# Attention weights and v in float32, and the product with v of a pair's two heads as float32 products in two column groups

## The chip, the cores and the metric

The kernel runs on one core of one Trainium2 chip. The metric is the device time of one execution in microseconds; three runs of the kernel before took 1297.36, 1299.44 and 1304.59 us, median 1299.44 us. A core has a matrix engine (PE, with its weight loads shown as PEld), a vector engine (DVE), an activation engine (ACT), a general engine (POOL) and a queue that issues DMAs (SP). Each engine runs its own instructions in order. Matrix products land in PSUM, eight banks of 128 partitions by 512 float32 values; all other tiles lie in SBUF.

## The reference, cut to what matters

Two layers, each attention and then a gated MLP, on 512 positions of width 1024; 16 heads of width 64. Layer 0 uses stick-breaking attention, layer 1 forgetting attention (a softmax with decay). In both, a causal matrix of weights `a` (or `p`) of each head multiplies that head's `v`:

```python
def stick_breaking_attention(q, k, v):
    ...
        z = jnp.einsum('bhqd,bhkd->bhqk', qb, kb).astype(jnp.float32) * scale
        ...
        a = jnp.where(strict, jnp.exp(log_beta + after), 0.0)
        outs.append(jnp.einsum('bhqk,bhkd->bhqd', a.astype(vb.dtype), vb))
...
def reference(x, c, w_mod, ...):
    for i in range(DEPTH):
        ...
        qkv = jnp.einsum('bsd,de->bse', h, w_qkv[i])
        q, k, v = (split_heads(t) for t in jnp.split(qkv, 3, axis=-1))
        ...
        o = jnp.einsum('bse,ed->bsd', merge_heads(o), w_o[i])
        x = x + gt_a[:, None, :] * rmsnorm(o, g_mix_post[i])
        ...
```

All is float32.

## The kernel before, in words

Almost every product is made of parts. A float32 tile is split (`split`, L190 to L193) into a high part of a reduced type (`fp32r`), written by ACT, and a low part, the difference, written by DVE or POOL. `mm3` (L264 to L268) then issues three products, high by high, low by high and high by low, into one bank.

Each layer's attention works through 16 heads in 8 pairs (`attention`, L529). In step h the scores of head h are made: four score products for query blocks of 128 rows, each in two parts (`scores`, L388), from which ACT, DVE and POOL make the weights (`stick` L391 to L401: two sigmoids on ACT, a scan on DVE at L399, a product on POOL or DVE at L400; `fox` L403 to L415 in layer 1). The head before, h-1, is turned meanwhile: `transposed` (L417) lets PE transpose its weights into four banks `pa` (L424) of 512, 384, 256 and 128 columns, one for each block kb of 128 key positions, and `split` makes high and low parts `ah` and `al` of them. Then `weighted` (L434) multiplies with v: the four v tiles hold for each head 64 high and 64 low columns, 128 in all, as the stationary operand; the moving operand is `ah` (L439) and then `al` (L440). So the bank `po` holds the product with v's high part in 64 partitions and with its low part in the other 64; ACT copies one half out (L444), DVE adds the other (L445) into `of`, and after a pair's second head `split` makes `oh` and `ol` of it, which `project` later multiplies with w_o.

PE's and SP's orders are those of the program text; the order of ACT, DVE and POOL is set by a scheduler when the program is built. Between these steps PE is given other work in small units by a `Filler` (L508): queries and keys of later pairs (`proj`, tile `pqk`), later v (`values`, tile `pv`), and the first products with w_o. The table `UNITS` says how many units stand in each step h, and the calls of `fill` in `attention` spread them in twelfths over the step. In layer 0 a second stream, `Background`, makes the next modulation columns on DVE from weights `wm` that DMAs bring (`acc`, L143); its DVE instructions stand between those of the attention. The v tiles come from `keep_values` (L464), for the first two groups of layer 0 at the end of `begin`, for the others in `values`. Most tiles of 128 by 512 (`slot`) share 44 rooms.

Of the kernel before, what the change touches and what calls it, by code (L numbers as in the profile page):

```python
# [8 lines left out]
F32 = mybir.dt.float32  # L9
# [3 lines left out]
ALU = mybir.AluOpType  # L13
AX = mybir.AxisListType

P = 128
D = 1024
S = 512
NT = S // P
ND = D // P  # L20
NH = 16
HD = 64
# [15 lines left out]
def trunk(ctx, tc, x, c, w_mod, b_mod, g_mix_pre, g_mix_post, w_qkv, w_o, w_fg, b_fg,  # L38
          g_ffn_pre, g_ffn_post, w_gate, w_up, w_conv, b_conv, w_down, out):
    nc = tc.nc  # L40
# [6 lines left out]
    def nm(s):  # L47
        serial[0] += 1
        return f"{s}_{serial[0]}"

    def bank(s="b"):
        return pp.tile([P, 512], F32, tag="bank", name=nm(s), bufs=8)

    def slot(s, dt=F32R):
        return sb.tile([P, 512], dt, tag="slot", name=nm(s), bufs=NS)
# [59 lines left out]
    def conv_columns():  # L115
        ps = bank("pcol")
        for l in range(DEPTH):
            nc.tensor.transpose(ps[:, P * l : P * l + 88], rowsB[:88, P * l : P * l + P], idn[:88, :88])
        for l in range(DEPTH):
            nc.vector.tensor_copy(colB[l], ps[:, P * l : P * l + 88])  # L120
        yield
# [69 lines left out]
    def split(hi, lo, src, engine=None):  # L191
        nc.scalar.copy(hi, src)  # L192
        (engine or nc.vector).tensor_tensor(lo, src, hi.bitcast(F32), op=ALU.subtract)  # L193
# [147 lines left out]
    def proj(l, p, j, ht, scale, res, parts=((0, S),)):  # L341
        wh, wl = ws.need((l, "qk", p, j))
        ps = bank("pqk")
        for c0, c1 in parts:
            for d in range(ND):
                ds_ = slice(d * P, (d + 1) * P)
                mm3(ps[:, c0:c1], (wh[:, ds_], wl[:, ds_]), block(ht, d, c0, c1), d == 0, d == ND - 1)
                if c1 - c0 == S or d % 2:
                    yield
        res[p, j] = queries(ps, scale) if j == 0 else keys(ps, kl[p % 2])  # L350

    A, B = slice(0, HD), slice(HD, P)
    kl = []

    def queries(ps, scale):

        res = slot("qa"), slot("qb")
        for x_, own in zip(res, (A, B)):
            nc.scalar.activation(x_[own], ps[own], AF.Copy, scale=scale)
        for x_, own, other in ((res[0], A, B), (res[1], B, A)):  # L360
            nc.vector.scalar_tensor_tensor(x_[other], ps[own], scale, x_[own].bitcast(F32), op0=ALU.mult, op1=ALU.subtract)
        return res
# [20 lines left out]
    def scores(l, hd, qb, q, k):  # L383
        n = (qb + 1) * P
        qs = slice(qb * P, n)
        ps = bank("ps")
        for i in range(2):
            nc.tensor.matmul(ps[:, :n], q[hd][:, qs], k[hd][i][:, :n], start=i == 0, stop=i == 1)  # L388
        return ps, n

    def stick(ps, n):  # L391


        bt = slot("bt", F32)
        om = slot("om", F32) if n > MULN else ps
        nc.gpsimd.memset(bt[:, n - 1 : n], 0.0)
        nc.scalar.activation(bt[:, : n - 1], ps[:, : n - 1], AF.Sigmoid)
        nc.scalar.activation(ps[:, :n], ps[:, :n], AF.Sigmoid, scale=-1.0)
        nc.vector.tensor_tensor_scan(om[:, :n][:, ::-1], ps[:, :n][:, ::-1], zid[:, S - n :][:, ::-1], 0.0, op0=ALU.mult, op1=ALU.add)  # L399
        (nc.gpsimd if n > MULN else nc.vector).tensor_tensor(bt[:, : n - 1], bt[:, : n - 1], om[:, 1:n], op=ALU.mult)  # L400
        return bt  # L401

    def fox(ps, qb, cum):  # L403

        n = (qb + 1) * P
        t = slot("fx", F32)[:, :n]
        e = t if n > MULN else ps[:, :n]
        m, s, r = tiny("mx"), tiny("sm"), tiny("rc")
        nc.vector.tensor_tensor_reduce(
            e.rearrange("p (b k) -> p b k", k=P), ps[:, :n].rearrange("p (b k) -> p b k", k=P), cum(qb),  # L410
            1.0, BIG, op0=ALU.add, op1=ALU.min, accum_out=m)
        nc.scalar.activation(e, e, AF.Exp, scale=-1.0, bias=m, accum_out=s)
        nc.vector.reciprocal(r, s)
        nc.vector.tensor_scalar(t, e, r, None, op0=ALU.mult)
        return t  # L415

    def transposed(probs):  # L417

        res = {}
        for kb in range(NT):  # L420
            n = (NT - kb) * P
            ps = bank("pa")
            for qb in range(NT - 1, kb - 1, -1):
                nc.tensor.transpose(ps[:, (qb - kb) * P : (qb - kb + 1) * P], probs[qb][:, kb * P : (kb + 1) * P], idn)  # L424
            if kb == 1:
                shared = slot("ah"), slot("al")
            hi, lo = (slot("ah"), slot("al")) if kb in (0, 2) else shared
            o = 384 if kb == 3 else 0
            hi, lo = hi[:, o : o + n], lo[:, o : o + n]
            split(hi, lo, ps[:, :n])  # L430
            res[kb] = (hi, lo)
            yield res

    def weighted(h, vt, at, o):  # L434

        po = bank("po")
        for kb in range(NT):
            lhs = by_head(vt[h // 4, kb])[:, h % 4, :]
            nc.tensor.matmul(po[:, kb * P :], lhs, at[kb][0], start=kb == 0, stop=False)  # L439
            nc.tensor.matmul(po[:, kb * P :], lhs, at[kb][1], start=False, stop=kb == NT - 1)  # L440
            yield
        hi, lo, f = o
        own, other = ((A, B), (B, A))[h % 2]
        nc.scalar.copy(f[own], po[other])  # L444
        nc.vector.tensor_tensor(f[own], po[own], f[own], op=ALU.add)  # L445
        if h % 2:
            split(hi, lo, f)

    def by_head(v):

        return v.rearrange("p (h e) -> p h e", h=4)

    def values(l, g, t, ht, vt):

# [7 lines left out]
        keep_values(ps[:, :256], g, t, vt)  # L462

    def keep_values(ps, g, t, vt):  # L464
        vt[g, t] = slot("v")
        dst = by_head(vt[g, t])
        split(dst[:, :, :HD], dst[:, :, HD:], ps.rearrange("p (h e) -> p h e", h=4))

    def forget(ht):

# [54 lines left out]
    def drain(g):  # L525
        for _ in g:
            pass

    def attention(l, qk, vt, ot, filler, units, bg):  # L529


        get = cums_of.get(l)
        late, cums = None, {}
        for h in range(NH + 1):
            p, hd = divmod(h, 2)
            done = [0, 0]

            def fill(n=1):
                done[0] += n
                u = (units[h] * min(done[0], 12) + 11) // 12 - done[1]  # L540
                done[1] += u
                filler.run(u)

            if h < NH and hd == 0:
                ot.append((slot("oh"), slot("ol"), slot("of", F32)))
            if get and h < NH:
                for i in range(h, min(h + 2, NH)):
                    if i not in cums:
                        cums[i] = get(i)
            probs, at = {}, None  # L550
            turned = transposed(late[0]) if late else None
            for qb in range(NT - 1, -1, -1):
                if h < NH:
                    ps, n = scores(l, hd, qb, qk[p, 0], qk[p, 1])
                    probs[qb] = stick(ps, n) if l % 2 == 0 else fox(ps, qb, cums[h])
                    fill()
                if turned:
                    at = next(turned)
                    fill()
            fill(2)  # L560
            if late:
                drain(turned)
                for i, _ in enumerate(weighted(late[1], vt, at, ot[late[1] // 2])):
                    if i % 2:
                        fill()
            fill(12)
            late = (probs, h)
            with tc.high_priority(offset=-100):
                bg.step(3 if h > 1 else 0)


    def begin(vt, qk):
# [41 lines left out]
        part, xt, acc, H = {}, {}, [], S // 2  # L614
# [92 lines left out]
        for t in range(NT):  # L707
            n = t + 1
# [29 lines left out]
        for j in range(ND):  # L738
            n = j + 1
# [17 lines left out]
        qk[0, 0] = queries(acc[4], 0.125)  # L757
        qk[0, 1] = keys(acc[6], kl[0])
        ws.upto(1)
        for g in range(2):  # L760
            for t in range(NT):
                keep_values(acc[t][:, 256 * g : 256 * g + 256], g, t, vt)
        qk[1, 0] = queries(acc[5], 0.125)
        return ht

# [1 line left out]
    for l in range(DEPTH):  # L767
# [35 lines left out]
        gens, ot = [], []  # L803
        for p in range(1, NPAIR):
            if (l, p) == (0, 3):
                gens.append(conv_columns())
            gens += [proj(l, p, j, ht, s, qk) for j, s in ((0, scale), (1, None)) if (p, j) not in qk]
            if p % 2 == 0 and (p // 2, 0) not in vt:
                gens += [values(l, p // 2, t, ht, vt) for t in range(NT)]
        gens += [project(t, ps_) for ps_ in (range(3), range(3, 5)) for t in range(2)] + [project(2, range(3))]  # L810
        filler = Filler(gens)
# [63 lines left out]
        for f in range(2, NF):  # L875
            g, u = bank("pgu"), bank("pgu")
# [67 lines left out]
```

## Time and profile before

| | us |
|---|---|
| median of three runs | 1299.44 |
| the profiled execution, its own time | 1295.07 |
| its span, first to last instruction | 1293.3 |
| PE busy | 1245.4 |
| DVE busy | 801.4 |
| ACT busy | 618.4 |
| POOL busy | 277.7 |

Layer 0's attention lies at about 85 to 275 us of the span, layer 1's at about 690 to 895 us, and the MLPs at 330 to 690 and from 930 us on. Busy times of PE count a product as longer than its place in the pipe: the ends of products are modelled, so the distance between two starts is the price of one product in a row. Idle time of an engine is given with what released it; where an engine runs in order, an instruction that waits holds up all that stand behind it.

### The profile page before, as it was taken

The page shows a single profiled execution, that of the slowest core. Times are in us where ns is not written, and L with a number is a line of the kernel's source. Part 1 is how long each engine was busy: PE and PEld are TensorE (multiplying, and loading weights), DVE is VectorE, ACT ScalarE, POOL GpSimd, SP SyncE. Part 2 cuts the span into 40 slices and gives each one's busy share as a digit, 9 for nine tenths or more (in the row PEclk, how much of TensorE's full clock was granted, in tenths as well). Part 3 has the DMA queues.
Part 4 walks back from the last instruction along what each step waited for, and adds up shares of the span by engine and source line. Part 5 has one row for each costly group of instructions (what it writes and reads, how often), then busy time and mean ns, then how long its engine had stood idle before and what let it go on. Part 6 is the DMA issues. An engine that isn't in the chain of part 4 may idle for free.

```text
span 1293.3 us, 17081 instructions
## 1 busy us (share of the span) xinstructions
PE 1245.4 (96%) x6244; PEld 1048.1 (81%) x6244; DVE 801.4 (62%) x1447; ACT 618.4 (48%) x1182; POOL 277.7 (21%) x302
## 2 busy tenths in 40 slices
PE   5899998999999999999999999999999999999997
PEld 3677878789888888888887889987888888888886
DVE  7878898856878887422363766776685444442233
ACT  5576666757333333311365665675743333332121
POOL 3665444620000000000113654452100000000000
PEclk9999999999999999999999999999999999999999
DMA  8662534231577776333403433332273333333231
GB/s 266 211 192 86 169 115 140 82 113 41 190 244 243 242 229 215 98 98 98 150 16 93 154 103 110 115 100 81 65 226 108 95 95 97 98 98 98 98 98 66
DMA packets 174857, 169.19 MB, mean 131 GB/s; under 512 B 6937, under 2 KB 151729, under 8 KB 174773
## 3 DMA queue, kind: packets, MB, share of 16 engines
q1 hardware_dynamic: 174596, 168.04, 41.3%
q8 instruction: 49, 0.80, 0.2%
q14 instruction: 36, 0.29, 0.1%
q10 hardware_dynamic: 176, 0.07, 0.0%
HBM read 165.92 MB, written 2.16 MB: 130 GB/s over the span
## 4 chain that ended last, share of the span: by engine, by line
PE 74%; DVE 12%; ACT 5%; DMA 4%; issue 3%; POOL 2%; SPq 0%; DVEq 0%; POOLq 0%; ACTq 0%
PE pgu L267 11%; PE pgu L266 11%; PE pgu L268 11%; PE pd L266 6%; PE pd L268 6%; PE pd L267 6%; PE pqk L266 3%; PE pqk L268 3%; PE pqk L267 3%; PE ps L388 2%; PE pa L424 2%; DMA wm<-in_w_mod_dram 2%; PE pv L267 2%; PE pv L266 2%; PE pv L268 2%
## 5 line engine op out<-in xcount | busy, mean ns | idle before, releaser
L192 ACT CAST wh<-wf 128x1024 fp32r<-128x1024 f32 (+2 forms) x178 | 185.3, 1041 | 313.8 <-PE pgu L267 140.6
L193 DVE TENSOR_TENSOR wl<-wf,wh 128x1024 fp32r<-128x1024 f32 x122 | 149.2, 1223 | 215.8 <-ACT wh L192 213.6
L267 PE MATMUL pgu<-htl,wh 128*128 128x512 f32 (+1 forms) x736 | 276.4, 376 | 0.4 <-DVE htl L328 0.3
L266 PE MATMUL pgu<-hth,wh 128*128 128x512 f32 (+1 forms) x736 | 276.3, 375 | 0.0
L268 PE MATMUL pgu<-hth,wl 128*128 128x512 f32 (+1 forms) x736 | 276.2, 375 | 0.0
L267 PEld LDWEIGHTS pgu<-htl,wh 128*128 128x128 f32 x736 | 138.5, 188 | 25.6 <-DVE htl L328 0.8
L193 POOL TENSOR_TENSOR wl<-wf,wh 128x1024 fp32r<-128x1024 f32 (+3 forms) x56 | 132.1, 2363 | 124.8 <-ACT wh L192 115.4
L266 PEld LDWEIGHTS pgu<-hth,wh 128*128 128x128 f32 x736 | 138.5, 188 | 25.1
L268 PEld LDWEIGHTS pgu<-hth,wl 128*128 128x128 f32 x736 | 138.5, 188 | 25.1
L279 POOL TENSOR_TENSOR r<-v,mhalf 128x1 f32<-128x1 f32 x32 | 17.9, 558 | 447.8 <-DVE v L275 447.8
L266 PE MATMUL pd<-wh,yh 128*128 128x512 f32 x288 | 112.0, 389 | 0.0
L267 PE MATMUL pd<-wl,yh 128*128 128x512 f32 x288 | 112.0, 389 | 0.0
L268 PE MATMUL pd<-wh,yl 128*128 128x512 f32 x288 | 112.0, 389 | 0.0
L143 DVE SCALAR_TENSOR_TENSOR acc<-wm,csil,acc 128x1024 f32<-128x1024 f32 x74 | 97.4, 1316 | 16.6 <-DMA wm<-in_w_mod_dram 16.0
L266 PE MATMUL pqk<-hth,wh 128*128 128x512 f32 (+1 forms) x240 | 100.6, 419 | 0.1
L268 PE MATMUL pqk<-hth,wl 128*128 128x512 f32 (+1 forms) x240 | 94.0, 392 | 0.4 <-POOL wl L193 0.4
L267 PE MATMUL pqk<-htl,wh 128*128 128x512 f32 (+1 forms) x240 | 93.6, 390 | 0.0
L856 ACT ACTIVATE cv<-cv 128x512 f32<-128x512 f32 x44 | 27.8, 632 | 102.7 <-DVE cv L855 98.2
L266 PE MATMUL pv<-wh,hth 128*128 128x256 f32 (+1 forms) x224 | 71.0, 317 | 0.8 <-ACT hth L663 0.4
L267 PE MATMUL pv<-wl,hth 128*128 128x256 f32 (+1 forms) x224 | 67.8, 303 | 0.9 <-POOL wl L193 0.9
L268 PE MATMUL pv<-wh,htl 128*128 128x256 f32 (+1 forms) x224 | 67.8, 303 | 0.0
L192 ACT CAST ah<-pa 128x128 fp32r<-128x128 f32 (+3 forms) x128 | 53.7, 427 | 21.0 <-PE pa L424 20.3
(199 smaller groups left out, 2442.8 us busy)
## 6 DMA issues: line engine op xcount, KB each, us to landing
wm<-in_w_mod_dram SPq DMA_DIRECT2D x80, 512.0 KB, 4.8
wf<-in_w_ffn_gate_dram SPq DMA_DIRECT2D x44, 512.0 KB, 4.1
wf<-in_w_ffn_up_dram SPq DMA_DIRECT2D x44, 512.0 KB, 3.7
wf<-in_w_ffn_down_dram SPq DMA_DIRECT2D x44, 512.0 KB, 3.5
wf<-in_w_qkv_dram SPq DMA_DIRECT2D x41, 512.0 KB, 3.8
wm<-in_w_mod_dram SPq DMA_DIRECT2D x32, 256.0 KB, 4.2
wf<-in_w_o_dram SPq DMA_DIRECT2D x16, 512.0 KB, 3.4
cum<-cumd SPq DMA_DIRECT2D x16, 512.0 KB, 4.3
```

The source lines that it names most:

```text
L143: nc.vector.scalar_tensor_tensor(acc, w, csil[:, d : d + 1], acc, op0=ALU.mult, op1=ALU.add)
L192: nc.scalar.copy(hi, src)
L193: (engine or nc.vector).tensor_tensor(lo, src, hi.bitcast(F32), op=ALU.subtract)
L266: nc.tensor.matmul(ps, ah, bh, start=first, stop=False)
L267: nc.tensor.matmul(ps, ah, bl, start=False, stop=False)
L268: nc.tensor.matmul(ps, al, bh, start=False, stop=last)
L279: nc.gpsimd.tensor_tensor(r, v, mhalf, op=ALU.pow)
L388: nc.tensor.matmul(ps[:, :n], q[hd][:, qs], k[hd][i][:, :n], start=i == 0, stop=i == 1)
L424: nc.tensor.transpose(ps[:, (qb - kb) * P : (qb - kb + 1) * P], probs[qb][:, kb * P : (kb + 1) * P], idn)
L856: nc.scalar.activation(a, a, AF.Silu)
```

## The change

The weights and v are no longer split. `transposed` copies each bank `pa` into a float32 tile `at` (ACT alone). `keep_values` copies v as float32, 512 columns, that is eight heads, to a tile. `weighted` now runs once for a pair, after its second head: for each key block it issues two float32 products, one for each head, with 64 columns of v as the stationary operand and `at` as the moving one; the first head's result goes to partitions 0 to 63 of the bank `po` and the second's to 64 to 127, with the tile position (0, 0) or (0, 64). `split` then makes `oh` and `ol` straight from the bank. The copy and the addition into `of` and the tile itself are gone, as are the two calls of `fill` between the products.

```diff
             if kb == 1:
-                shared = slot("ah"), slot("al")
-            hi, lo = (slot("ah"), slot("al")) if kb in (0, 2) else shared
+                shared = slot("at", F32)
+            t = shared if kb % 2 else slot("at", F32)
             o = 384 if kb == 3 else 0
-            hi, lo = hi[:, o : o + n], lo[:, o : o + n]
-            split(hi, lo, ps[:, :n])
-            res[kb] = (hi, lo)
+            res[kb] = t[:, o : o + n]
+            nc.scalar.copy(res[kb], ps[:, :n])
             yield res
 
-    def weighted(h, vt, at, o):
+    def weighted(p, vt, at, o):
 
         po = bank("po")
         for kb in range(NT):
-            lhs = by_head(vt[h // 4, kb])[:, h % 4, :]
-            nc.tensor.matmul(po[:, kb * P :], lhs, at[kb][0], start=kb == 0, stop=False)
-            nc.tensor.matmul(po[:, kb * P :], lhs, at[kb][1], start=False, stop=kb == NT - 1)
-            yield
-        hi, lo, f = o
-        own, other = ((A, B), (B, A))[h % 2]
-        nc.scalar.copy(f[own], po[other])
-        nc.vector.tensor_tensor(f[own], po[own], f[own], op=ALU.add)
-        if h % 2:
-            split(hi, lo, f)
...
+            for hd in range(2):
+                e = P * (p % 4) + HD * hd
+                nc.tensor.matmul(po[HD * hd : HD * hd + HD, kb * P :], vt[p // 4, kb][:, e : e + HD], at[hd][kb],
+                                 start=kb == 0, stop=kb == NT - 1, tile_position=(0, HD * hd))
+        split(*o, po)
...
     def keep_values(ps, g, t, vt):
-        vt[g, t] = slot("v")
-        dst = by_head(vt[g, t])
-        split(dst[:, :, :HD], dst[:, :, HD:], ps.rearrange("p (h e) -> p h e", h=4))
+        if (g // 2, t) not in vt:
+            vt[g // 2, t] = slot("v", F32)
+        o = 256 * (g % 2)
+        nc.scalar.copy(vt[g // 2, t][:, o : o + 256], ps)
...
             if late:
                 drain(turned)
-                for i, _ in enumerate(weighted(late[1], vt, at, ot[late[1] // 2])):
-                    if i % 2:
-                        fill()
+                if hd == 0:
+                    weighted(p - 1, vt, ats, ot[p - 1])
+                    ats = {}
             fill(12)
...
-        for g in range(2):
-            for t in range(NT):
-                keep_values(acc[t][:, 256 * g : 256 * g + 256], g, t, vt)
+        for t in range(NT):
+            vt[0, t] = slot("v", F32)
+            nc.scalar.copy(vt[0, t], acc[t])
```

The first place is PE in layer 0 at the products with v of the first pair. In the kernel before they stand once for each head; these are those of the pair's second head (`po` is the bank they add into, `ah` and `al` the parts of the turned weights, `v` the four v tiles, `pqk` a filler's bank):

```order
L439 MATMUL po_1135<-ah_1043,v_774 128x512
L440 MATMUL po_1135<-al_1044,v_774 128x512
L439 MATMUL po_1135<-ah_1067,v_777 128x384
L440 MATMUL po_1135<-al_1068,v_777 128x384
L266 MATMUL pqk_1118<-hth_107,wh_891 128x512
L267 MATMUL pqk_1118<-htl_108,wh_891 128x512
L268 MATMUL pqk_1118<-hth_107,wl_892 128x512
L439 MATMUL po_1135<-ah_1099,v_780 128x256
L440 MATMUL po_1135<-al_1100,v_780 128x256
L439 MATMUL po_1135<-ah_1067,v_783 128x128
L440 MATMUL po_1135<-al_1068,v_783 128x128
```

In the changed kernel PE has at this place the only run of the pair, with the two heads' tiles `at` in turn:

```order
L439 MATMUL po_1092<-at_903,v_774 64x512
L439 MATMUL po_1092<-at_1007,v_774 64x512
L439 MATMUL po_1092<-at_925,v_776 64x384
L439 MATMUL po_1092<-at_1029,v_776 64x384
L439 MATMUL po_1092<-at_945,v_778 64x256
L439 MATMUL po_1092<-at_1059,v_778 64x256
L439 MATMUL po_1092<-at_925,v_780 64x128
L439 MATMUL po_1092<-at_1029,v_780 64x128
L266 MATMUL pqk_1076<-hth_107,wh_874 128x512
```

Sixteen products for the pair, each into all 128 partitions, have become eight, each into 64; the first head's run has moved to the second's, and the filler's unit that stood inside the run stands behind it.

The second place is DVE in layer 0 while the first head is turned and the second head's weights are made (`om` and `ps` of L399 are the scans, `al` the low parts of the turned weights, `acc` the background sum, `bt` the weights). The kernel before has:

```order
L399 SCALAR_TENSOR_TENSOR om_906<-ps_902,zid 128x512
L193 TENSOR_TENSOR al_921<-pa_915,ah_920 128x512
L143 SCALAR_TENSOR_TENSOR acc_1151<-wm_1157,csil,acc_1151 128x1024
L399 SCALAR_TENSOR_TENSOR om_931<-ps_927,zid 128x384
L193 TENSOR_TENSOR al_945<-pa_940,ah_944 128x384
L143 SCALAR_TENSOR_TENSOR acc_1151<-wm_1160,csil,acc_1151 128x1024
L399 SCALAR_TENSOR_TENSOR ps_951<-ps_951,zid 128x256
L193 TENSOR_TENSOR al_967<-pa_963,ah_966 128x256
L400 TENSOR_TENSOR bt_954<-bt_954,ps_951 128x255
L399 SCALAR_TENSOR_TENSOR ps_970<-ps_970,zid 128x128
L193 TENSOR_TENSOR al_945<-pa_982,ah_944 128x128
L400 TENSOR_TENSOR bt_973<-bt_973,ps_970 128x127
```

The changed kernel has on DVE at this place:

```order
L399 SCALAR_TENSOR_TENSOR om_889<-ps_885,zid 128x512
L143 SCALAR_TENSOR_TENSOR acc_1106<-wm_1109,csil,acc_1106 128x1024
L399 SCALAR_TENSOR_TENSOR om_912<-ps_908,zid 128x384
L143 SCALAR_TENSOR_TENSOR acc_1106<-wm_1112,csil,acc_1106 128x1024
L399 SCALAR_TENSOR_TENSOR ps_930<-ps_930,zid 128x256
L143 SCALAR_TENSOR_TENSOR acc_1106<-wm_1115,csil,acc_1106 128x1024
L400 TENSOR_TENSOR bt_933<-bt_933,ps_930 128x255
L399 SCALAR_TENSOR_TENSOR ps_947<-ps_947,zid 128x128
L400 TENSOR_TENSOR bt_950<-bt_950,ps_947 128x127
```

The four subtractions are gone; the scans and background sums stay in turn.

More of the change, by code (lines that the diff above doesn't have):

```diff
@@ L425, in transposed @@
             if kb == 1:
-                shared = slot("ah"), slot("al")
-            hi, lo = (slot("ah"), slot("al")) if kb in (0, 2) else shared
+                shared = slot("at", F32)
+            t = shared if kb % 2 else slot("at", F32)
             o = 384 if kb == 3 else 0
-            hi, lo = hi[:, o : o + n], lo[:, o : o + n]
-            split(hi, lo, ps[:, :n])
-            res[kb] = (hi, lo)
+            res[kb] = t[:, o : o + n]
+            nc.scalar.copy(res[kb], ps[:, :n])
             yield res
-    def weighted(h, vt, at, o):
+    def weighted(p, vt, at, o):
         po = bank("po")
         for kb in range(NT):
-            lhs = by_head(vt[h // 4, kb])[:, h % 4, :]
-            nc.tensor.matmul(po[:, kb * P :], lhs, at[kb][0], start=kb == 0, stop=False)
-            nc.tensor.matmul(po[:, kb * P :], lhs, at[kb][1], start=False, stop=kb == NT - 1)
-            yield
-        hi, lo, f = o
-        own, other = ((A, B), (B, A))[h % 2]
-        nc.scalar.copy(f[own], po[other])
-        nc.vector.tensor_tensor(f[own], po[own], f[own], op=ALU.add)
-        if h % 2:
-            split(hi, lo, f)
-    def by_head(v):
-        return v.rearrange("p (h e) -> p h e", h=4)
+            for hd in range(2):
[3 more added lines that the diff above has]
+        split(*o, po)
     def values(l, g, t, ht, vt):
@@ L532, in attention @@
         get = cums_of.get(l)
-        late, cums = None, {}
+        late, ats, cums = None, {}, {}
         for h in range(NH + 1):
@@ L544, in attention @@
             if h < NH and hd == 0:
-                ot.append((slot("oh"), slot("ol"), slot("of", F32)))
+                ot.append((slot("oh"), slot("ol")))
             if get and h < NH:
@@ L549, in attention @@
                         cums[i] = get(i)
-            probs, at = {}, None
+            probs = {}
             turned = transposed(late[0]) if late else None
@@ L557, in attention @@
                 if turned:
-                    at = next(turned)
+                    ats[late[1] % 2] = next(turned)
                     fill()
@@ L807, in trunk @@
             gens += [proj(l, p, j, ht, s, qk) for j, s in ((0, scale), (1, None)) if (p, j) not in qk]
-            if p % 2 == 0 and (p // 2, 0) not in vt:
+            if p % 2 == 0 and p >= (4 if l == 0 else 2):
                 gens += [values(l, p // 2, t, ht, vt) for t in range(NT)]
```

## The prediction

> **What bounds the kernel now.** I read the page first: span, busy times, then busy times by stretch, then who waits for whom on PE, then the rows of single gaps.
>
> ```profile
> span 1293.3 us, 17081 instructions
> PE 1245.4 (96%) x6244; PEld 1048.1 (81%) x6244; DVE 801.4 (62%) x1447; ACT 618.4 (48%) x1182; POOL 277.7 (21%) x302
> ```
>
> PE works through nearly the whole span, so a change pays only where PE stands still or in what PE itself does. The busy time of each engine by stretch shows where it stands still (columns: stretch, length, busy PE, PEld, DVE, ACT, POOL with counts, granted clock, DMA share, GB/s). The rows are layer 0's attention, its MLP, and layer 1's attention:
>
> ```profile
> 85.00:275.00 190.00, 174.25 (x967) 147.72 (x966) 157.43 (x276) 120.96 (x263) 97.52 (x130) 0.97 0.37 120
> 330.00:690.00 360.00, 358.89 (x1650) 298.10 (x1649) 219.22 (x320) 134.73 (x206) 15.58 (x17) 1.00 0.50 160
> 690.00:895.00 205.00, 201.30 (x1176) 173.68 (x1176) 138.72 (x392) 129.79 (x299) 102.23 (x80) 1.00 0.37 117
> ```
>
> PE is idle for 190 - 174.25 = 15.75 us in layer 0's attention, where DVE is busy 157.43 of 190 us (83%); for 3.7 us in layer 1's, where DVE is at 68%; for 1.1 us in the MLP. PE's waits in the first of these stretches, and then the three of layer 1 that bear on this change, say for whom:
>
> ```profile
> PE ps L388 <- DVE om L399: 9.1, 5, 4.8
> PE po L440 <- DVE al L193: 2.7, 4, 1.1
> PE pa L424 <- DVE om L399: 2.4, 2, 1.3
> PE ps L388 <- POOL kh L379: 0.8, 1, 0.8
> PE po L439 <- DVE om L399: 0.3, 1, 0.3
> ...
> PE pa L424 <- DVE al L193: 0.6, 1, 0.6
> PE po L266 <- DVE al L193: 0.2, 1, 0.2
> PE po L440 <- DVE al L193: 0.2, 1, 0.2
> ```
>
> Nearly all of it is DVE being late: with the scan (`om`) or with the low part `al` itself. And idle time costs twice. Three pieces of 30 us, each around a cluster of such gaps, have a granted clock of 0.94 where other stretches have 1.00:
>
> ```profile
> 90.00:120.00 30.00, 25.85 (x122) 20.50 (x121) 27.41 (x43) 17.26 (x35) 16.62 (x20) 0.94 0.43 139
> 150.00:180.00 30.00, 24.98 (x136) 20.59 (x134) 26.24 (x36) 16.79 (x36) 11.87 (x14) 0.94 0.55 181
> 210.00:240.00 30.00, 27.40 (x161) 24.30 (x160) 22.82 (x51) 22.06 (x49) 14.04 (x20) 0.94 0.16 53
> ```
>
> Each loses 0.06 x 30 = 1.8 us of PE's speed.
>
> **Part 1: what DVE and ACT are rid of.** The groups by line and shape (count, then busy us, mean ns):
>
> ```profile
> L193 DVE TENSOR_TENSOR al<-pa,ah 128x512 fp32r<-128x512 f32 x32 | 21.7, 677 | 0.9 <-ACT ah L192 0.9
> L193 DVE TENSOR_TENSOR al<-pa,ah 128x384 fp32r<-128x384 f32 x32 | 17.3, 541 | 0.3
> L193 DVE TENSOR_TENSOR al<-pa,ah 128x256 fp32r<-128x256 f32 x32 | 13.2, 413 | 1.7 <-ACT ah L192 1.6
> L193 DVE TENSOR_TENSOR al<-pa,ah 128x128 fp32r<-128x128 f32 x32 | 8.9, 279 | 0.6 <-ACT ah L192 0.6
> L445 DVE TENSOR_TENSOR of<-po,of 64x512 f32<-64x512 f32 x32 | 22.0, 687 | 26.5 <-ACT of L444 26.2
> L193 DVE TENSOR_TENSOR v<-pv,v 128x256 fp32r<-128x256 f32 x32 | 12.7, 414 | 3.1 <-ACT v L192 3.0
> L444 ACT COPY of<-po 64x512 f32<-64x512 f32 x32 | 18.6, 582 | 39.5 <-PE po L440 39.2
> ```
>
> DVE loses 21.7 + 17.3 + 13.2 + 8.9 + 22.0 + 12.7 = 95.8 us of work, nearly half of it in layer 0's attention, where (61.1 + 22.0)/2 = 41.6 us go besides v's; its 157 us become about 115. ACT loses 18.6 us; its copies of `pa` and v stay, with float32 in place of fp32r as output, taken at the same price. None of this is time by itself: it lies beside PE's stream. What counts is which gaps of PE close.
>
> The four waits of L440 for `al` go (2.7 us): the product needs only ACT's copy, on which `al` had to wait too. For the scans I look at what DVE did before a gap:
>
> ```profile
> 98.32 1.21 DVE L399 TENSOR_TENSOR_SCAN om<-ps,zid 128x512 f32<-128x512 f32 x1
> 99.45 0.66 DVE L193 TENSOR_TENSOR al<-pa,ah 128x512 fp32r<-128x512 f32 x1
> 100.03 1.27 DVE L143 SCALAR_TENSOR_TENSOR acc<-wm,csil,acc 128x1024 f32<-128x1024 f32 x1
> 101.23 0.94 DVE L399 TENSOR_TENSOR_SCAN om<-ps,zid 128x384 f32<-128x384 f32 x1
> ```
>
> DVE runs without a pause and PE waits 1.1 us for the scan of 98.32. One `of` (0.69) and four `al` (1.91 in all) stood ahead of it: 2.6 us go, so this gap closes. I take the other short waits for a scan to close the same way. The longest does not:
>
> ```profile
> 156.88 1.90 DVE L143 SCALAR_TENSOR_TENSOR acc<-wm,csil,acc 128x1024 f32<-128x1024 f32 x1 [1.35 <-DMA wm<-in_w_mod_dram]
> 158.71 2.84 DVE L193 TENSOR_TENSOR ol<-of,oh 128x512 fp32r<-128x512 f32 x1
> ...
> 164.05 0.39 PE L388 MATMUL ps<-kh,qb 128*128 128x128 f32 x1 [4.82 <-DVE om L399]
> ```
>
> Here DVE itself waited for the background's DMA, then for nothing that is removed. I leave all 4.8 us of it, and its dip of the clock. Closed: 2.7 + (9.1 - 4.8) + 2.4 + 0.3 = 9.7 us of gaps, two dips of three, 3.6 us, and the 0.6 + 0.2 + 0.2 = 1.0 us of layer 1 that `al` causes: **-14.3 us**. The bounds are -2.7 us (only the `al` waits go) and 15.75 + 5.4 + 3.7 = -24.9 us (everything goes). What is late next is PE's own stream; ACT, with 121 - 9 = 112 us of some 176, has room.
>
> **Part 2: the products.** Before, from their starts in the timeline (start, duration, ...):
>
> ```profile
> 773.21 0.39 PE L439 MATMUL po<-ah,v 128*128 128x512 f32 x1
> ...
> 774.01 0.40 PE L266 MATMUL pqk<-hth,wh 128*128 128x512 f32 x1
> ...
> 774.71 0.28 PE L439 MATMUL po<-ah,v 128*128 128x256 f32 x1
> ...
> 775.11 0.45 PE L266 MATMUL pqk<-hth,wh 128*128 128x512 f32 x1
> ```
>
> A head's eight products take 0.80 + 0.40 = 1.20 us, a pair's 2.40, and these are 2 x 2 x 1280 columns, 0.47 ns a column. No row shows a float32 product that adds up. If it is as exact as float32, it must hold what the high and low parts hold, four part-products where the kernel before makes two (v's parts share one stationary tile): 4 x 0.47 = 1.88 ns a column, 2.40 us a head. The Trainium skill ("FP8 and Floating Point Precision", TensorE Precision Notes) puts true float32 at four passes, by which the sum would be the one worked out here; no run here shows it yet. If the two column groups work side by side, a pair costs 2.40 us, as before; one after the other, 4.80. The nearest row with a float32 operand is the transpose:
>
> ```profile
> 302.59 1.03 PE L319 MATMUL pt<-zid,xn 128*128 128x128 f32 x8
> 303.38 0.36 PE L266 MATMUL pgu<-hth,wh 128*128 128x256 f32 x1
> ```
>
> Eight take about 0.88 us (0.79, and 0.09 that the product behind them is late), 0.86 ns a column: by that a pair's 2560 columns take 2.20 us in turn and 1.10 side by side. So the ends are 1.10 and 4.80 us a pair, and two ways, one by each row, lead to 2.2 to 2.4. I take 2.40: **0 us**, with -1.3 x 16 = -21 and +2.4 x 16 = +38 us as ends.
>
> **Part 3: changing between the forms.** PE goes from 128-column products to 64-column ones and back, 2 x 16 times. The nearest row is the change from a transpose back to a product, the 0.09 us above: 32 x 0.09 = **+2.9 us**, between nothing and 32 x 0.16 (a product of 0.39 us by its row, of which 0.23 is its place in a row) = +5.1. The Trainium skill ("TensorEngine Tiling (Array Packing)", Key Properties) says that a change of the tiling mode drains TensorE; by the drain of 0.16 the sum would be 2.2 us worse.
>
> **Part 4: moves.** The first head's products move a head later, to the second's place. They issue no DMA and pass no queue. The added wait is that for both heads' copies: behind it on PE stand the filler and the next scores. The first head's copies are a head old, and the second's have five products ahead of the last that needs one; that, and the subtraction that is no longer in between, more than make up for the two fills that the run loses: 0 us. If the cover is gone, one ACT copy a pair, 0.58 us by L444's row, +9. In place of ACT copy, DVE addition, ACT, DVE comes ACT, DVE behind the products, which no PE wait above needs.
>
> **Sum.** -14.3 + 0 + 2.9 = -11.4 us, 1295.07 -> 1283.7 in terms of the profiled execution; that execution lies 4.4 us below the median of the runs, so for the median 1299.44 - 11.4 = **1288 us**.
>
> **Rivals.**
> 1. *The column groups work in turn* (the slower side). Everything is as above but a pair's products take 4.80 us: 1288 + 38 = 1326. For it: PE is one engine with one instruction stream, and no row of before has two products at once. Against it: the operands and halves of the bank are disjoint, and the two heads alternate, product by product. It decides from 0.71 us a pair (11.4/16): with less than 70% of the second head hidden there is no gain left. The Trainium skill speaks for this rival in "TensorE: Matmul & The Clock Gate", Part 3, What overlaps and what doesn't: a weight load overlaps a running product only where their row groups differ, and here the rows are shared; by that rule the time is this rival's. Against it stands the Trainium skill's table in the same Part 3, Measured speedup vs the span model, with three column tiles 2.38 times as fast as in turn; by it the forecast holds. No run here shows either.
> 2. *The gaps stay.* DVE stops being late but PE still waits, now for the background's DMA at `wm` (DVE stands in order behind it, as at 156.88) or for a partial overlap's loss: -2.7 + 2.9 = 0, 1299.6; from 1293 to 1306. For it: the 4.8 us gap began with that DMA. Against it: in layer 0's attention DVE waited for that DMA twice only:
>
> ```profile
> DVE acc L143 <- DMA wm<-in_w_mod_dram: 1.6, 2, 1.3
> ```
>
> 3. *Float32 products are as cheap as the transposes and side by side*: 1288 - 21 = 1267.
>
> That the change doesn't do what it says can be left out: the order of PE shows the eight 64-row products of each pair.
>
> **How the numbers follow.** Forecast 1288 (1280 to 1296): 0.52. Rival 1 (1308 to 1328): 0.25. Rival 2: 0.17. Rival 3: 0.06. The range 1278 to 1320 leaves out rival 3 and the upper half of rival 1, some 0.18. Half a per cent, 6.5 us, is about what a measurement can tell from no change; so faster is below 1293: most of the forecast, and rival 3: 0.54. Same, to 1306: rival 2 and the forecast's upper end: 0.18. Slower: rival 1 and the upper end of rival 2: 0.28.
>
> **What would show it.** The starts of a pair's eight products: 2.4 us from the first to the filler behind them says side by side, 4.8 in turn, 1.1 cheap. DVE busy near 706 us and ACT near 600. In layer 0's attention, PE idle near 6 us and one clock dip in place of three; no wait of L439 for DVE `al`. The distance from the product ahead of a run to its first row shows the change of form. I am wrong if the run takes over 3.1 us, or if waits for `om` stay above 6 us with DVE below 65% busy.

## The result, and the profile after

The changed kernel takes 1283.08 us (median of four runs, 1282.77 to 1283.68), the kernel before 1299.57 us (four runs, 1297.36 to 1304.59): a ratio of 0.9872 with a 95% interval of 0.9852 to 0.9892, 16.5 us less. The profiled execution took 1282.77 us, 12.3 us less than that of the kernel before, which lies 4.5 us below its median; a second trace of the kernel before, below, took 1300.49 us. Of the page after, the span and the busy times:

```profile
span 1280.9 us, 16845 instructions
PE 1237.8 (97%) x6244; PEld 1024.1 (80%) x6244; DVE 727.0 (57%) x1255; ACT 600.2 (47%) x1146; POOL 277.9 (22%) x302
```

DVE is rid of 74 us and ACT of 18 us. The busy times by stretch, columns as before, for the two attentions (by the end of layer 1's the changed kernel is some 12 us ahead):

```profile
85.00:275.00 190.00, 178.70 (x998) 141.66 (x998) 127.49 (x198) 117.83 (x255) 99.72 (x127) 0.98 0.40 127
690.00:895.00 205.00, 201.95 (x1175) 165.44 (x1175) 108.72 (x307) 119.22 (x286) 99.67 (x82) 1.00 0.39 121
```

DVE falls from 83% to 67% of the first stretch, PE's idle time from 15.75 to 11.3 us, and the granted clock rises from 0.97 to 0.98. PE's waits in that stretch, sum, times, longest:

```profile
PE pa L424 <- POOL bt L396: 4.6, 4, 2.5
PE ps L388 <- POOL kh L379: 2.0, 1, 2.0
PE pa L424 <- DVE bt L400: 1.5, 2, 1.1
PE pa L424 <- DVE ol L193: 1.2, 1, 1.2
PE pv L266 <- DVE om L399: 0.7, 1, 0.7
PE pa L424 <- DVE om L399: 0.6, 2, 0.4
```

The waits for the scan have shrunk from 11.8 us to 1.3, and those for `al` are gone. In their place PE waits for the weights `bt` themselves, mostly from POOL: PE comes to the transposes before they are made. In the longest of these waits (2.5 us, at 163.25 us) POOL makes the weights late because it first works through two instructions that make low parts of other weights, of matrices that a DMA brought:

```profile
156.69 5.68 POOL L193 TENSOR_TENSOR wl<-wf,wh 128x1024 fp32r<-128x1024 f32 x2
162.34 0.85 POOL L400 TENSOR_TENSOR bt<-bt,om 128x383 f32<-128x383 f32 x1
```

The scan that this product needs had ended on DVE at 158.69. The timeline at one pair's run of products:

```profile
98.12 0.40 PE L268 MATMUL pqk<-hth,wl 128*128 128x512 f32 x1
98.45 2.38 PE L439 MATMUL po<-at,v 128*64 128x512 f32 x16
100.75 0.50 PE L266 MATMUL pqk<-hth,wh 128*128 128x512 f32 x1
101.09 0.39 PE L267 MATMUL pqk<-htl,wh 128*128 128x512 f32 x1
```

Eight products stand as 16 rows, two for each. From the first start to the start behind the run it is 100.75 - 98.45 = 2.30 us, and so in 15 of the 16 pairs (2.90 in one that waited for a copy). The step into the run is 0.33 us where a product's place is 0.23, the step behind the next product 0.34.

Where the time went, by the starts of PE's rows in the timeline (us; idle time of PE in brackets):

| stage, from the first row of one to the first of the next | before | before, second trace | after |
|---|---|---|---|
| first `pv` to the first score of layer 0 | 55.6 (8.7) | 56.5 (7.0) | 54.3 (8.9) |
| layer 0, first score to first gate product | 227.5 (16.1) | 229.0 (16.5) | 219.0 (11.3) |
| layer 0, gate and up | 249.1 (0.4) | 250.8 (1.8) | 250.7 (1.8) |
| layer 1, first score to first gate product | 221.6 (2.3) | 222.7 (1.9) | 218.4 (1.6) |

Layer 0's attention stage gave 8.5 us, of which 4.8 are PE's idle time; layer 1's gave 3.2.

### The profile page after: what moved, and what is told of

The parts are those of the page before. It is cut to its first block, busy times and chain, and to the rows that moved or that the text cites. A ratio compares the mean times of both kernels' runs of the same rounds, so it can differ in the third digit from the quotient of the medians.

```text
span 1280.9 us, 16845 instructions
## 1 busy us (share of the span) xinstructions
PE 1237.8 (97%) x6244; PEld 1024.1 (80%) x6244; DVE 727.0 (57%) x1255; ACT 600.2 (47%) x1146; POOL 277.9 (22%) x302
## 4 chain that ended last, share of the span: by engine, by line
PE 75%; DVE 8%; DMA 6%; issue 3%; ACT 3%; POOL 2%; SPq 1%; DVEq 0%; POOLq 0%; ACTq 0%
PE pgu L267 11%; PE pgu L268 11%; PE pgu L266 11%; PE pd L267 6%; PE pd L268 6%; PE pd L266 6%; DMA wm<-in_w_mod_dram 3%; PE pqk L266 3%; PE pqk L267 3%; PE pqk L268 3%; PE po L439 2%; PE pa L424 2%; PE ps L388 2%; PE po L266 2%; PE po L268 1%
## 5 line engine op out<-in xcount | busy, mean ns | idle before, releaser
L143 DVE SCALAR_TENSOR_TENSOR acc<-wm,csil,acc 128x1024 f32<-128x1024 f32 x74 | 98.3, 1329 | 32.3 <-DMA wm<-in_w_mod_dram 31.6
L266 PEld LDWEIGHTS pd<-wh,yh 128*128 128x128 f32 x288 | 54.1, 188 | 11.3
```

Source lines behind the costliest of these rows:

```text
L143: nc.vector.scalar_tensor_tensor(acc, w, csil[:, d : d + 1], acc, op0=ALU.mult, op1=ALU.add)
L266: nc.tensor.matmul(ps, ah, bh, start=first, stop=False)
```

## The experiments

Ratios are to runs of the kernel before on the same chip, beside each experiment, with 95% intervals; the changed kernel's is 0.9872 (0.9852 to 0.9892).

**Do the two column groups work side by side?** First the order of the products, head by head:

```diff
-        for kb in range(NT):
-            for hd in range(2):
+        for hd in range(2):
+            for kb in range(NT):
```

> The changed kernel with a pair's eight products in another order: all four of the first head, then all four of the second. Nothing else differs. Theory A (the two column groups work side by side, but PE starts products in order, so that only neighbours in the stream overlap): a run of the pair takes about twice the 2.30 us of the changed kernel's trace, 4.3 to 4.6 us, and the time rises by some 32 to 37 us to about 1317. Theory B (a float32 product of 64 columns just costs half, two parts' price, and nothing overlaps): the run stays at 2.30 us and the time at 1283.

Then both heads in one group, each with a bank:

```diff
-        po = bank("po")
+        po = bank("po"), bank("po")
...
-                nc.tensor.matmul(po[HD * hd : HD * hd + HD, kb * P :], vt[p // 4, kb][:, e : e + HD], at[hd][kb],
-                                 start=kb == 0, stop=kb == NT - 1, tile_position=(0, HD * hd))
-        split(*o, po)
+                nc.tensor.matmul(po[hd][:HD, kb * P :], vt[p // 4, kb][:, e : e + HD], at[hd][kb],
+                                 start=kb == 0, stop=kb == NT - 1, tile_position=(0, 0))
+        f = slot("of", F32)
+        nc.scalar.copy(f[A], po[0][A])
+        nc.scalar.copy(f[B], po[1][A])
+        split(*o, f)
```

> The changed kernel with both heads' products in the first column group, each head into a bank of its own, alternating as in the changed kernel; two ACT copies a pair (0.58 us each) bring the halves together. Theory A (the groups are what overlaps): 4.3 to 4.6 us a run, about 1317 us. Theory B (a float32 product of 64 columns costs half, no overlap by groups): 2.30 us a run, about 1284 us.

They took 1302.41 us (1.003, 1.0012 to 1.0047) and 1310.77 us (1.008, 1.006 to 1.01). A run of each in the timeline, head by head and then in one group:

```profile
175.24 3.93 PE L439 MATMUL po<-at,v 128*64 128x512 f32 x16
179.10 0.50 PE L266 MATMUL pqk<-hth,wh 128*128 128x512 f32 x1
```

```profile
127.47 4.52 PE L439 MATMUL po<-at,v 128*64 128x512 f32 x16
131.92 0.50 PE L266 MATMUL pqk<-hth,wh 128*128 128x512 f32 x1
```

3.86 and 4.45 us a run against 2.30: theory A. In two groups the products run 4.45 / 2.30 = 1.93 times as fast, but only where neighbours in the stream are of different groups; head by head only the seam overlaps, which saves 0.59 us. The runs alone would add 16 x 1.56 = 25 and 16 x 2.15 = 34 us; the times rose by 19 and 28, in part because the longer stream also covers gaps (PE's idle time in layer 0's attention stage falls from 11.3 to 8.5 and 8.9 us).

**Is it the products or the relief?** The subtraction of the weights back, in the changed kernel, read by nothing:

```diff
             res[kb] = t[:, o : o + n]
             nc.scalar.copy(res[kb], ps[:, :n])
+            nc.vector.tensor_tensor(low[:, o : o + n], ps[:, :n], res[kb], op=ALU.subtract)
```

> The changed kernel with the four subtractions for each head (bank less its copy) put back on DVE; their result is read by nothing. DVE gets some 61 us back, PE's stream stays that of the changed kernel. If the gain is DVE's relief (my part 1), most of it goes: about 1292, between 1289 and 1297, the waits of PE for the scan are back and layer 0 has two or three dips of the clock again. If the gain comes from the shape of the products themselves, it stays within 2 us of 1283.

And the kernel before without it:

```diff
-            split(hi, lo, ps[:, :n])
-            res[kb] = (hi, lo)
+            nc.scalar.copy(hi, ps[:, :n])
+            res[kb] = (hi, hi)
```

> The kernel before without the low part of the weights: the second product of each key block reads the high part again, so the low part's contribution is left out and the high part's counted twice. PE has the same products as before, DVE has 61 us less. If the gain is DVE's relief: about 1288, between 1284 and 1291. If it is the products: 1297 to 1300.

They took 1285.85 us (0.989, 0.9863 to 0.9917) and 1287.57 us (0.99, 0.9872 to 0.9927). The second is as the relief theory had it: PE's products are those of before and most of the gain is there. The first is not: with the subtractions back (61 us by their mean durations, 49 us more of DVE's busy time), the time cannot be told from that of the changed kernel. So the subtractions are enough to explain most of the gain when they go, and cost next to nothing when they come back. Something else that the change removed had to be at work as well; all of it went back, `al`, the subtraction of v, and the copy and addition of `of`:

```diff
+            nc.vector.tensor_tensor(low[:, o : o + n], ps[:, :n], res[kb], op=ALU.subtract)
...
+        nc.vector.tensor_tensor(slot("vl")[:, :256], ps, vt[g // 2, t][:, o : o + 256], op=ALU.subtract)
...
+        f = slot("of", F32)
+        for own in (A, B):
+            nc.scalar.copy(f[own], po[own])
+            nc.vector.tensor_tensor(f[own], po[own], f[own], op=ALU.add)
         split(*o, po)
```

> The changed kernel with all the work that the change took from DVE and ACT put back, its results read by nothing: the subtractions of the weights and of v on DVE, and for each head a copy of 64 partitions on ACT and an addition on DVE. DVE should be near 800 us busy again. Theory 1 (it is DVE's total work that made PE wait): the time goes back to the kernel before, 1296 to 1300. Theory 2 (it is that PE's products no longer stand behind the low part, and a pair's run needs only ACT's copies; DVE's load matters little): 1285 to 1290.

1304.43 us (1.0041, 1.0021 to 1.006). The whole gain is gone and a little more, with the new products in place. But what went back is more than what the change took. In the kernel before, a bank `po` was free after one copy and one addition, and `split` read `of` in SBUF; here one bank is held through two copies, two additions and the split. So this run alone does not say that the form of the products is worth nothing. The kernel before without `al` says more: its products, its copies and additions and its split of v are those of before, and all of these together leave it 4.5 us above the changed kernel, with overlapping intervals.

**Which part of the relief?** The copy and addition alone (the last four added lines above), and the subtraction of the weights alone, but twice:

> The changed kernel with only the copy of 64 partitions on ACT and the addition on DVE put back for each head, their results read by nothing: 22 us more of DVE work, and DVE in order stands behind ACT's copy (8 to 15 us of such waits in layer 0 in the runs that have it). Theory 1 (what counts is DVE's work together with the time it stands blocked; PE suffers only above some 80% of layer 0's attention): here about 76%, so 1283 to 1286. Theory 3 (it is this blocking pair that costs, whatever the load): most of the 16.5 us is back, 1293 or more.

> The changed kernel with the subtraction of the weights put back twice: 122 us more on DVE than in the changed kernel, no copy and addition for each head. Theory 1 (work and blocked time together, a knee near 80%): DVE is past 88% in layer 0's attention, so 1297 to 1310. Theory 3 (the blocking pair): it is not here, so at most 1290.

1297.76 us (0.9984, 0.9974 to 0.9994) and 1291.38 us (0.9936, 0.9921 to 0.9952). Not the amount of work: the additions with their copies cost 14.7 us and the subtractions twice 8.3, though by the pages DVE's busy time rises by 25 us with the first (752.2 for 727.0) and by 95 with the second (821.8). The windows view of 70 to 290 us shows it: DVE is busy 152.26 of 220 us with the additions, 194.59 with the subtractions twice, and the first is the slower:

```profile
70.00:290.00 220.00, 200.52 (x1086) 160.30 (x1085) 152.26 (x230) 140.82 (x305) 110.24 (x144) 0.95 0.39 125
```

```profile
70.00:290.00 220.00, 204.60 (x1136) 162.27 (x1136) 194.59 (x356) 141.00 (x311) 110.65 (x145) 1.00 0.41 129
```

The rows also differ in the granted clock, 0.95 and 1.00. By PE's starts layer 0's attention stage takes 231.3 us with the additions and 221.6 with the subtractions twice, with 19.5 and 15.4 us of it idle: so 4.1 of the 9.7 us between them are idle time, and most of the rest goes with the clock (an estimate: 0.05 of 220 is 11 us). PE's longest waits in this stretch are 5.8 and 1.9 us; whether long waits lower the clock, no run tried.

In the trace with the additions PE waits for `ol`, the last reader of the bank `po`. PE's waits, and one of them followed in the timelines of PE, DVE and ACT:

```profile
PE pa L424 <- DVE ol L193: 7.6, 3, 5.8
PE ps L388 <- DVE ol L193: 4.3, 1, 4.3
```

```profile
106.85 1.28 DVE L143 SCALAR_TENSOR_TENSOR acc<-wm,csil,acc 128x1024 f32<-128x1024 f32 x1 [4.69 <-DMA wm<-in_w_mod_dram]
108.05 0.68 DVE L444 TENSOR_TENSOR of<-po,of 64x512 f32<-64x512 f32 x1
...
112.28 0.69 DVE L193 TENSOR_TENSOR ol<-po,oh 128x512 fp32r<-128x512 f32 x1
```

```profile
108.76 0.58 ACT L443 COPY of<-po 64x512 f32<-64x512 f32 x1 [7.00 <-DVE of L444]
109.95 1.04 ACT L146 CAST ah<-acc 128x1024 fp32r<-128x1024 f32 x1 [0.61 <-DVE acc L143]
111.02 0.59 ACT L192 CAST oh<-po 128x512 fp32r<-128x512 f32 x1
```

```profile
113.12 0.45 PE L424 MATMUL pa<-zid,bt 128*128 128x128 f32 x1 [5.82 <-DVE ol L193]
```

A background sum waits 4.7 us for its DMA on DVE; the addition stands behind it in order; ACT's second copy waits 7.0 us for the addition; the cast and `ol` come behind; and only then is the bank free that PE needs for the next transposes, 5.8 us late. To tell the held bank from the work, the same copies and additions were put behind the split, where they read the high part in SBUF:

```diff
         split(*o, po)
+        f, x_ = slot("of", F32), o[0].bitcast(F32)
+        for own in (A, B):
+            nc.scalar.copy(f[own], x_[own])
+            nc.vector.tensor_tensor(f[own], x_[own], f[own], op=ALU.add)
```

> The run before last but one put a copy on ACT and an addition on DVE for each head between the pair's products and the split, and took 1298 us: PE waited 12.9 us for DVE's `ol`, the last reader of the bank `po`. Here the same two instructions for each head stand behind the split and read the finished high part in SBUF, so that they hold no bank; their results are read by nothing. If the price was the bank held by a chain of four hops between ACT and DVE: 1283 to 1287. If it was the added work, or engines blocked in order wherever the pair stands: 1293 or more.

(By the rows above the wait for `ol` in layer 0 is 7.6 + 4.3 = 11.9 us, not the 12.9 of that text.) 1286.03 us (0.9882, 0.9864 to 0.9899): not to be told from the changed kernel. So it is not the added work. Nor is it simply that DVE stands blocked behind ACT: from 70 to 290 us DVE waits 16.3 us for ACT ahead of the additions and `ol` where they hold the bank (13.6 + 2.7), and 12.5 us where they don't (all ahead of `ol`). What differs is PE's wait for `ol`, 11.9 and 3.6 us; its idle time in layer 0's attention stage is 19.5 and 13.1 us. At the place followed above, the background sum waits for its DMA in all three kernels, 4.7 us with the additions, 4.5 with them off the bank and 4.4 in the changed kernel; PE is then late by 5.8, 3.2 and 1.2 us. It is the bank held by a chain of hops that turns a wait of DVE into one of PE.

**What is late next?** The 384-column product of weights on DVE, and then the key's other half on ACT:

```diff
-        (nc.gpsimd if n > MULN else nc.vector).tensor_tensor(bt[:, : n - 1], ...
+        (nc.gpsimd if n > 384 else nc.vector).tensor_tensor(bt[:, : n - 1], ...
...
-            nc.gpsimd.tensor_scalar(hi[other], hi[own].bitcast(F32), 1.0, 1.0, op0=ALU.mult, op1=ALU.mult)
+            nc.scalar.copy(hi[other], ps[own])
```

> The changed kernel with the 384-column product of weights in layer 0 (L400) on DVE in place of POOL, where it takes about 0.55 us in place of 1.05. In the changed kernel's trace PE waits 4.6 us for weights from POOL. If that chain is what is late now: faster by 2 to 4 us, about 1280. If DVE just becomes late in its place: no change within 1.5 us, with waits for the scan back.

> As the last, and the other head's half of the key's high part is written by ACT from the bank (0.58 us) in place of POOL (L379), on which PE waited 2.0 us in layer 0 and 1.4 us at the start of layer 1. If these waits lie on PE's path: another 2 to 3 us, about 1277. If ACT, in order, is then late with the sigmoids: no better than the last.

1285.62 us (0.9898, 0.9853 to 0.9943) and 1283.57 us (0.9883, 0.9848 to 0.9918): nothing gained. The first one's waits show why:

```profile
PE pa L424 <- DVE bt L400: 7.5, 7, 2.9
PE ps L388 <- DVE om L399: 3.0, 1, 3.0
```

PE waits for the same weights from the other engine. The last is the filler's place:

```diff
+            yield
         split(*o, po)
...
-                    weighted(p - 1, vt, ats, ot[p - 1])
+                    for i, _ in enumerate(weighted(p - 1, vt, ats, ot[p - 1])):
+                        if i % 2:
+                            fill()
```

> The changed kernel with the filler's units put back between the second and third key block of a run and behind the run's end, as the kernel before had them: PE changes form once or twice more for each pair. If a change there and back costs 0.2 us, as the changed kernel's trace has it: +3 to +6 us where PE is the bound, 1285 to 1289. If it costs nothing: 1283.

1281.01 us (0.985, 0.9833 to 0.9867; 1278.04 to 1282.13 in four runs, all below the changed kernel's, though the intervals of the two ratios overlap). Most pairs now enter and leave the new form twice, each time with the same steps of 0.33 us in the timeline, and yet the time did not rise to the 1285 to 1289 us that this price would give: PE's idle time in layer 0's attention stage falls from 11.3 to 7.8 us. This is the lowest median of all versions tried.

**The kernel before once more.**

> The kernel before once more, for a second trace. Its runs spread from 1294 to 1303 us, those of the changed kernel by 1 us. If the spread is PE's waits in layer 0's attention, this trace differs from the first there and nowhere else by more than 1 us.

1300.49 us. It is longer than the first trace in all four stages of the table, by 0.9 to 1.7 us, not in one: a miss. Much of the difference goes with the granted clock, 0.989 over the whole span for 0.994 in the first trace; 0.005 of 1293 us is 6.5 us, and the spans differ by 5.4. The other runs of this kernel go the same way: of 46 beside the experiments the four above 1303 us have a clock of 0.988 to 0.991, the four below 1295 us one of 0.992 to 0.994. The changed kernel's four have 0.994 or 0.995. So by the same estimate some 5 of the 16.5 us between the medians go with the clock (0.995 for a median of 0.991). Why the clock differs from run to run of one kernel is open.

## Why the prediction was right, point by point

**Part 2, the products: right.** A pair takes 2.30 us, priced 2.40. Four part-products is the right count: in one group 4.45 us for 2560 columns is 1.74 ns a column, 3.9 times the 0.45 ns of an `fp32r` product (0.23 us for 512). By the Trainium skill's four passes ("FP8 and Floating Point Precision", TensorE Precision Notes) it would be 4: the runs agree. The transposes' 0.86 ns a column in turn gave nearly the same sum, 2.20 us, by luck; in one group there is no such price.

**Rival 1, in turn: refuted, and its price nearly right.** 4.45 us a run where the rival had 4.80, and 1310.77 us in place of 1326: the forecast on which the rival stands was 5 us high, a run is 0.35 us cheaper, and the longer stream covers gaps. The rule behind it, from the Trainium skill ("TensorE: Matmul & The Clock Gate", Part 3, What overlaps and what doesn't), that weight loads overlap running products only where row groups differ, does not hold here. The profile of the kernel before showed that already: with all rows shared, loads were busy for 81% of the span and products for 96%, so they overlapped. The table in the same part of the Trainium skill has 2.38 for three column tiles; this case has 1.93 for two.

**Part 3, the change of form: right.** 0.10 us into the run and 0.11 behind it, 16 x 0.21 = 3.4 us, priced 2.9. A drain of 0.16 each way, as the Trainium skill's rule ("TensorEngine Tiling (Array Packing)", Key Properties) was worked out, is above the rows.

**Part 1, -14.3 us: near in sum, wrong in the way.** The forecast of -11.4 us stands beside -12.3 in the profiled executions and -16.5 in the medians; the difference of these two is the first trace, which lies below its median. That the sum came out is in part luck. The step that failed is the count of DVE's work ahead of a gap ("one `of` (0.69) and four `al` (1.91 in all) stood ahead of it: 2.6 us go, so this gap closes"), which makes the subtractions most of the relief. The runs show that put back once they cost nothing that can be measured, and twice 8.3 us. The reading of that gap was off as well: PE's wait of 1.1 us ends at 102.2 us, behind the scan that starts at 101.23, not the one of 98.32.

The waits named did go, 2.7 us for `al` and 10.5 of 11.8 for the scan. But "what is late next is PE's own stream" was wrong: POOL's and DVE's `bt` and POOL's `kh` came next, and idle time in layer 0's attention stage fell by 4.8 us, not by 9.7, to 11.3 where 6 was forecast. Of the clock's three dips two went, as forecast: in windows of 10 us the granted clock at 100 to 110 and at 210 to 220 us rose from 0.83 to 1.00. But at 160 to 170 us it fell from 0.83 to 0.66, so the clock gave some 1.7 us, not 3.6. DVE's busy time fell by 74 us, not by 95.8 to 706, because its rows overlap: in the prediction's own lines the scan of 98.32 lasts 1.21 us, to 99.53, and the next instruction starts at 99.45. A sum of mean durations counts such time twice.

**Part 4: a term put at nothing.** The prediction wrote of the chain "ACT copy, DVE addition, ACT, DVE" that "no PE wait above needs" it, and put its shortening at nothing. Put back in a longer form, it costs 14.7 us, because its last reader holds a bank. What it cost as it stood in the kernel before was not measured. PE's waits there name the scan and `al`, never the chain, as the prediction had it; but DVE stood 26.2 us waiting for ACT's copies at the addition, by the row of L445, and the prediction counted only the 22.0 us of the additions themselves. Without `al` the old chain is still there, and the kernel is only 4.5 us slower than the changed one. In the kernels' traces layer 0's attention stage is 226.7 to 233.8 us where copy and addition read the bank (the kernel before twice, without `al`, with `of` back, with all back) and 217.2 to 224.5 us in the others on two groups that alternate, even with the subtractions twice (221.6). What the kernel before without `al` gained lies elsewhere, as in layer 1's stage with 218.8 us for 221.6.

So this much is shown: most of the gain is DVE's and ACT's relief and not the products, since the kernel before without `al` has it with its old products. How the 16.5 us divide is not shown. The parts do not add up: with either `al` or the chain gone most of the gain is there, and this is only measured, not explained.

The two fills were put at nothing; back in their place the median is 2 us lower, which the intervals do not separate from nothing.

**Rivals 2 and 3.** The gaps partly stayed, as rival 2 had it, but mostly with another releaser than the background's DMA. DVE waits for that DMA more than before (31.6 us in the page's row of `acc`, 16.0 before), and of PE's waits the 1.2 us for `ol` stand behind it. Rival 3 is out by the 2.30 us.

## What to carry to other kernels

Price what an instruction holds, not only how long it takes: short copies and additions between two in-order engines cost the changed kernel more (14.7 us) than almost four times as much DVE work that held a bank only for its own time (8.3), because a bank that PE needs was released behind the whole chain. Column groups on PE pay only if neighbours in the stream alternate. When a gap is put down to one engine's work, put back just that work before believing it. And see that what is put back is what was taken: here the chain put back held its bank longer than the one that was removed.

## What was not expected of the hardware

A float32 product stands as two rows in the trace, 64 columns wide with 618 ns for 512 columns each; two column groups bring 1.93 of 2 with eight products alternating (2.30 us against 4.45), and 1.15 head by head (3.86).
